# Split-weight slots of 4,128 bytes in place of 4,096 in a one-core encoder layer

## The chip, the core and the metric

The kernel runs on one core of a Trainium2 chip. The metric is the device time of one execution in microseconds, of which the median over several runs is given; lower is better. A matmul of this kernel is one TensorE (PE) instruction with a stationary operand of up to 128 x 128 elements, loaded ahead of it by an instruction that the profile keeps apart as PEld, and a moving operand of up to 512 columns.

## What is computed

One layer of an encoder over 256 tokens with 2,048 features, in float32:

```python
x = LN(ALPHA * x + 0.5 * swiglu(x, ffn1_w_gate, ffn1_w_up, ffn1_w_down))     # 2048 -> 5632 -> 2048
x = LN(ALPHA * x + (sigmoid(x @ w_gate[0] + b_gate[0]) * (diff_attention(x) @ w_branch_a)
                    + sigmoid(x @ w_gate[1] + b_gate[1]) * (dsa_attention(x) @ w_branch_b)) @ w_mix_out)
x = LN(ALPHA * x + memory_attention(x, mem))                                 # 4 heads over 256 memory tokens
x = LN(ALPHA * x + 0.5 * swiglu(x, ffn2_w_gate, ffn2_w_up, ffn2_w_down))
```

where `swiglu(x, g, u, d) = (silu(x @ g) * (x @ u)) @ d`. Nearly all of the work is products of 256 tokens with weight matrices that are read once from HBM.

## The kernel before, in words

Every product is made of float32r matmuls. To keep float32 accuracy each operand is split into a high part and a low part, and each product is the sum of three matmuls (`mm3`, lines 172 to 175): high times high (L173), high of the activations times low of the weights (L174), and low of the activations times high of the weights (L175). The activations, transposed (tile `xT`, or `hh` and `hl`, `ring`, `memT`, `mq`), are the stationary operand, 128 x 128. The weights (tiles `whi` and `wlo`) are the moving operand, 512 columns of them.

The weights come in units of 128 partitions x 1,024 float32, which is two k-tiles of 512 columns. SP loads a unit into one of four `raw` tiles (line 182), ACT copies it to `whi` with rounding to float32r (line 169), and DVE writes `wlo = raw - whi` (line 170). A split unit lies in a slot, a pair of `whi` and `wlo`, until both token tiles have used it: 2 token tiles x 2 k-tiles x 3 matmuls, 12 in all. There are six slots in the pool `wspl` throughout, four more in the pool `wx1` during the first feed-forward and two more in `wx2` during the second. `Feed` decides in program order which slot the next unit takes (the first pool with a free one) and how far ahead it is split. The order of all instructions is written out by the program (`manual_schedule`); nothing reorders them.

The tiles of a pool lie one behind the other in each partition of SBUF, and pools lie one behind the other too: `base` (with `xT`), `wraw` (`raw`), `wspl`, `stat`, and behind that the tiles of the current stage. So the length of a slot's tile sets the start address of every tile behind it. A slot's two tiles are 1,024 x 4 = 4,096 bytes each, a multiple of 256.

Of the kernel before, what the change touches and what calls it, by code (L numbers as in the profile page):

```python
# [16 lines left out]
P = 128  # L17
# [30 lines left out]
class Task:  # L48
    """Emission of a chain of dependent instructions in steps, between products."""

# [33 lines left out]
class Feed:  # L84
    """The weight units in the order of their use: loaded and split ahead of it."""

# [38 lines left out]
    def pump(self, count=99):  # L125
        """Splits ahead, while there is room."""
        while count and self.nsplit < len(self.plan):
            if self.plan[self.nsplit][3] is None and not any(self.slots.values()):
                return
            if self.nth[self.nsplit] > self.pulled + min(AHEAD, RAMP[0] + self.pulled // RAMP[1]):  # L130
                return
            self._split()
            count -= 1
# [16 lines left out]
def tile_encoder_layer(ctx, tc, a, out):  # L150
# [25 lines left out]

# [1 line left out]
    def load(src, width, cut):  # L178
# [8 lines left out]
    def split_unit(raw, width, into, cut, slot):  # L187
        if into is not None:
            hi, lo = into()
            raw = raw.rearrange("p (k t) -> p k t", t=T)  # L190
            w = 4 // cut
        else:
            hi = spl_pools[slot].tile([P, UNIT], F32R, name="whi")
            lo = spl_pools[slot].tile([P, UNIT], F32R, name="wlo")
            w = width // cut
        for i in range(cut):
            c = slice(i * w, (i + 1) * w)
            split(hi[:, c], lo[:, c], raw[:, c])
        return hi, lo
# [5 lines left out]
    @contextmanager  # L205
    def more_slots(name, bufs):
        """More room for split units, inside; its last ones are in use by then, and none is taken."""
        with tc.tile_pool(name=name, bufs=bufs) as pool:
            spl_pools[name] = pool
            feed.slots[name] = bufs  # L210
            yield
# [71 lines left out]
    def product(lhs, w, n, kts, lead=0, trail=0, after=None):  # L283
        """The two token tiles of lhs[K, tokens].T @ W[:, chunk n], over k-tiles kts of W: token tile 0
        ahead of tile 1 by `lead` units at the start and by `trail` at the end."""
        dst = [acc(), acc()]
        nu = len(kts) // KT
        held = {}

        def half(t, i):  # L290
            if i not in held:
                held[i] = feed.pull((w, n, kts[i * KT][1] // KT))
            unit_mm(lhs, dst, held[i], [kts[i * KT + j][0] for j in range(KT)], t, i == 0, i == nu - 1)
            if t == 1:
                feed.free(held.pop(i))
                if i < lead:
                    feed.pump(1)
                elif i - nu + trail == 1:
                    feed.pump(1)
            if i == nu - 1 and after is not None:  # L300
                after(t, dst[t])

        for t in range(2):
            for i in range(lead):
                half(t, i)
                tasks.tick()
        for i in range(lead, nu - trail):
            half(0, i)
            half(1, i)
            tasks.tick()  # L310
        for t in range(2):
            for i in range(nu - trail, nu):
                half(t, i)
                tasks.tick()
        return dst
# [8 lines left out]
    def rsqrt(dst, src, scale, eps):  # L324
        """dst = (src * scale + eps) ** -0.5"""
        w = src.shape[-1]
        v = stat.tile([P, 8], F32, name="rsq")
        nc.vector.tensor_scalar(v[:, :w], src, scale, eps, op0=ALU.mult, op1=ALU.add)
        nc.gpsimd.tensor_tensor(dst, v[:, :w], neg_half[:, :w], ALU.pow)  # L329

    def blocks_T(src, width=NCOL):
        """The transposes of src's 128-column blocks."""
        p = tp()
        for b in range(width // P):
            nc.tensor.transpose(p[:, b * P:(b + 1) * P], src[:, b * P:(b + 1) * P], ident)  # L335
        return p

    def transposed(src, hi, lo, width=NCOL):
        """hi + lo = the transposes of src's 128-column blocks."""
        p = blocks_T(src, width)[:, :width]  # L340
        split(hi, lo, p.rearrange("p (b t) -> p b t", t=P) if len(hi.shape) == 3 else p)
# [13 lines left out]

# [1 line left out]
    def ln_vectors(pool, i):  # L357
# [20 lines left out]
    def gain_bias_T(dst, p, i, n):  # L378
        """dst = p's blocks, a feature to a partition, times the gain, plus the bias of layer norm i."""
        for b in range(4):  # L380
            k = 2 * i * KD + 4 * n + b
            bs = slice(b * P, (b + 1) * P)
            nc.scalar.activation(dst[:, bs], p[:, bs], AF.Identity, scale=lnT[:, k:k + 1],
                                 bias=lnT[:, k + KD:k + KD + 1])

    def ln_task(y, t, sts, i, xT, gb, scratch, keep, kinds, pause, stride):
        """y's tile t <- its layer norm i; xT <- the norm, transposed and split. A chunk gets its gain
        and bias before the transposes (A) or, a feature to a partition, behind them (B)."""
        mv, rstd = ln_moments(sts)
# [55 lines left out]
    def store_task(y, t, sts, i, gb, scratch):  # L445
        """The last layer norm of y's tile t, stored: three chunks on DVE, one on ACT and TensorE."""
        mv, rstd = ln_moments(sts)
# [32 lines left out]

# [1 line left out]
    def ffn(pre, pool, y, xT, sts, lead, end):  # L482
        """y <- ALPHA * y + 0.5 * SwiGLU(x); end(t) follows the last product of token tile t."""
        for gi, (c0, c1) in enumerate(FFN_GROUPS):
# [39 lines left out]

# [1 line left out]
    x1_dram = dram.tile([P, 2, D], F32, name="x1_dram")  # L526
# [39 lines left out]

# [1 line left out]
    with tc.tile_pool(name="att", bufs=1) as att:  # L568
# [6 lines left out]
        def cols_T(p, scale, wait=0):  # L575
            """A product's token tiles, transposed: [feature, block, token]."""
            r = ring()
# [13 lines left out]
        def rows(p):  # L591
            """A product's token tiles as they are: [token, tile, column]."""
            r = ring().rearrange("p s b t -> p s (b t)")
            for t in range(2):
                s = slice(t * NCOL, (t + 1) * NCOL)
                split(r[:, 0, s], r[:, 1, s], p[t])
            return r
# [38 lines left out]
        def softmax_exp(dist, slope, p):  # L636
            """exp(logits - their maximum) and the sums, for both token tiles."""
            e = att.tile([P, 384], F32, name="e", bufs=4)
# [9 lines left out]
        def probs_T(e):  # L648
            """[key, (keys 0-127: 256 tokens | keys 128-255: tokens 128-255)]"""
            pT = att.tile([P, 2, 384], F32R, name="pT", bufs=2)  # L650
            transposed(e, pT[:, 0, :], pT[:, 1, :], 384)
            return pT

# [1 line left out]
        def diff_head(q, k, v, b, g, r):  # L655
# [43 lines left out]
        def heads(head, args, count, period, after):  # L699
            """Starts a head every `period` steps, once the tasks `after` are through."""  # L700
            while not all(t.done for t in after):
# [25 lines left out]

# [1 line left out]
        iq0, _ = cols_T(w_in(9), 1.0)  # L729
# [61 lines left out]

# [1 line left out]
        cT = ring()  # L793
# [21 lines left out]
        def latents(g):  # L815
            """Keys [feature, head, token] and values [token, tile, (head, feature)] of heads 4g..4g+3."""
            k = ring()
# [17 lines left out]

# [1 line left out]
        def dsa_head(q, k, v, b, g, r):  # L837
# [25 lines left out]

# [1 line left out]
        def y_lhs(yT):  # L865
# [68 lines left out]
    with tc.tile_pool(name="mem", bufs=1) as pool:  # L934
# [20 lines left out]

# [1 line left out]
        def cols_T2(p, scale, name):  # L957
# [58 lines left out]

# [1 line left out]
    with more_slots("wx2", MORE[1]), tc.tile_pool(name="ffn2", bufs=1) as pool:  # L1018
# [51 lines left out]
def _units(w):  # L1070
    """[K, N] -> [N chunk, K group, partition, (k-tile, column)]"""
    k, n = w.shape
# [4 lines left out]
def _columns(x):  # L1077
    """[tokens, K] -> [partition, (k-tile, token)]"""
    t, k = x.shape
# [52 lines left out]
```

## Time and profile before

| what | value |
|---|---|
| median of three runs | 2293.91 us (2292.02 to 2294.64) |
| span of the profiled execution, first to last instruction | 2291.1 us |
| PE busy in the span | 2273.7 us, 99%, 10,408 matmuls |
| PEld busy | 1866.6 us, 81% |
| DVE busy | 1283.5 us, 56% |
| ACT busy | 1031.0 us, 45% |
| mean granted TensorE clock | 0.998 |
| HBM traffic | 431.29 MB read, 190 GB/s over the span |

The profiled execution has no time of its own beside its span. The span is 2.8 us under the median of the runs, which also hold the start and the end around it. Matmuls are pipelined: one lasts some 390 ns by its record, and the next starts long before it ends. So for PE the time from one start to the next counts, and not the duration.

### The profile page before, as it was taken

To read this page: it belongs to the slowest core of one execution; us is meant where nothing else is said; L and a number is where in the kernel's file an instruction comes from. 1 tells how busy PE (TensorE), PEld (TensorE's weight loads), DVE (VectorE), ACT (ScalarE), POOL (GpSimd) and SP (SyncE) were. 2 spreads that over 40 slices of the span, in tenths; PEclk is the share of its full clock that TensorE was granted. 3 is DMA by queue.
4 is the path that set the end of the run, shared out by engine and by line. 5 is a ranking of instruction groups with operands and counts; after the bars stand their busy time and mean duration, and the time that the engine had idled before them with its cause. 6 is when DMAs were issued, how large, how long until landed. Compare 5 with 4: busy or idle time off the path is not lost.

```text
span 2291.1 us, 27032 instructions
## 1 busy us (share of the span) xinstructions
PE 2273.7 (99%) x10408; PEld 1866.6 (81%) x10408; DVE 1283.5 (56%) x1458; ACT 1031.0 (45%) x1317; POOL 22.0 (1%) x36
## 2 busy tenths in 40 slices
PE   9999999999999999999999999999999999999998
PEld 7888888888888888888888888878888888888886
DVE  5544544554455766685655556786445445454554
ACT  5443344434443555655544444655443444434442
POOL 0000000000000100000000000000000000000000
PEclk9999999999999999999999999999999999999999
DMA  8866666666665655445566677547666666666662
GB/s 269 285 201 187 190 189 187 188 189 188 190 184 168 211 156 175 141 147 172 183 191 206 199 240 245 173 159 223 188 227 186 191 187 191 184 190 189 187 186 93
DMA packets 120592, 437.25 MB, mean 191 GB/s; under 512 B 13504, under 2 KB 13632, under 8 KB 119312
## 3 DMA queue, kind: packets, MB, share of 16 engines
q1 hardware_dynamic: 119520, 431.02, 60.9%
q0 software_dynamic: 944, 4.52, 0.6%
q8 instruction: 81, 1.33, 0.2%
q14 instruction: 47, 0.39, 0.1%
HBM read 431.29 MB, written 4.19 MB: 190 GB/s over the span
## 4 chain that ended last, share of the span: by engine, by line
PE 98%; issue 1%; DVE 1%; ACT 0%; DMA 0%; POOL 0%; SPq 0%; POOLq 0%; ACTq 0%
PE acc L173 31%; PE acc L175 31%; PE acc L174 31%; PE tp L335 2%; PE tp L173 1%; PE tp L174 1%; PE tp L175 0%; DMA raw<-in_ffn_w_gate 0%; ACT me L985 0%; DVE nm L981 0%; DVE wlo L170 0%; ACT whi L169 0%; POOL rstd L329 0%; DVE sts L479 0%; DVE y L477 0%
## 5 line engine op out<-in xcount | busy, mean ns | idle before, releaser
L170 DVE TENSOR_TENSOR wlo<-raw,whi 128x1024 fp32r<-128x1024 f32 (+1 forms) x787 | 959.1, 1222 | 861.8 <-ACT whi L169 856.6
L169 ACT CAST whi<-raw 128x1024 fp32r<-128x1024 f32 (+1 forms) x787 | 822.4, 1049 | 957.1 <-PE acc L175 910.4
L173 PE MATMUL acc<-whi,xT 128*128 128x512 f32 x2176 | 857.3, 394 | 2.0 <-ACT whi L169 2.0
L175 PE MATMUL acc<-whi,xT 128*128 128x512 f32 x2176 | 850.9, 391 | 0.0
L174 PE MATMUL acc<-wlo,xT 128*128 128x512 f32 x2176 | 850.4, 391 | 0.2 <-DVE wlo L170 0.2
L173 PEld LDWEIGHTS acc<-whi,xT 128*128 128x128 f32 x2176 | 409.0, 188 | 90.3 <-ACT whi L169 4.0
L175 PEld LDWEIGHTS acc<-whi,xT 128*128 128x128 f32 x2176 | 408.7, 188 | 88.4
L174 PEld LDWEIGHTS acc<-wlo,xT 128*128 128x128 f32 x2176 | 409.2, 188 | 87.0 <-DVE wlo L170 1.4
L173 PE MATMUL acc<-whi,hh 128*128 128x512 f32 x704 | 277.6, 394 | 0.0
L175 PE MATMUL acc<-whi,hl 128*128 128x512 f32 x704 | 276.9, 393 | 0.0
L174 PE MATMUL acc<-wlo,hh 128*128 128x512 f32 x704 | 276.7, 393 | 0.0
L175 PEld LDWEIGHTS acc<-whi,hl 128*128 128x128 f32 x704 | 132.2, 188 | 30.6
L174 PEld LDWEIGHTS acc<-wlo,hh 128*128 128x128 f32 x704 | 132.2, 188 | 30.3
L173 PEld LDWEIGHTS acc<-whi,hh 128*128 128x128 f32 x704 | 132.2, 188 | 30.1
L173 PE MATMUL acc<-whi,ring 128*128 128x512 f32 x144 | 57.4, 398 | 0.0
L174 PE MATMUL acc<-wlo,ring 128*128 128x512 f32 x144 | 56.8, 395 | 0.0
L175 PE MATMUL acc<-whi,ring 128*128 128x512 f32 x144 | 56.8, 395 | 0.0
L477 DVE SCALAR_TENSOR_TENSOR y<-y,acc 128x512 f32<-128x512 f32 x64 | 42.2, 680 | 18.4 <-PE acc L175 18.3
L170 DVE TENSOR_TENSOR hl<-tp,hh 128x512 fp32r<-128x512 f32 x44 | 28.4, 686 | 33.5 <-ACT hh L169 33.5
L169 ACT CAST hh<-tp 128x512 fp32r<-128x512 f32 x44 | 23.7, 590 | 49.0 <-PE tp L335 49.0
L644 ACT ACTIVATE e<-e,nm 128x128 f32<-128x128 f32 (+1 forms) x48 | 21.5, 448 | 45.6 <-DVE nm L643 44.6
L500 ACT ACTIVATE silu<-acc 128x512 f32<-128x512 f32 x44 | 26.2, 599 | 22.7 <-PE acc L175 22.6
(194 smaller groups left out, 1097.7 us busy)
## 6 DMA issues: line engine op xcount, KB each, us to landing
raw<-in_ffn_w_up SPq DMA_DIRECT2D x176, 512.0 KB, 4.2
raw<-in_ffn_w_down SPq DMA_DIRECT2D x176, 512.0 KB, 3.8
raw<-in_ffn_w_gate SPq DMA_DIRECT2D x175, 512.0 KB, 4.1
raw<-in_w_in SPq DMA_DIRECT2D x88, 512.0 KB, 3.6
raw<-in_w_gate SPq DMA_DIRECT2D x64, 512.0 KB, 4.2
raw<-in_w_mix_out SPq DMA_DIRECT2D x32, 512.0 KB, 4.2
raw<-in_w_branch_a SPq DMA_DIRECT2D x16, 512.0 KB, 4.1
raw<-in_w_branch_b SPq DMA_DIRECT2D x16, 512.0 KB, 4.2
```

The costliest lines, as they stand in the source:

```text
L169: nc.scalar.copy(hi, src)
L170: nc.vector.tensor_tensor(lo, src, hi.bitcast(F32), ALU.subtract)
L173: nc.tensor.matmul(dst, lh, rh, start=start, stop=False)
L174: nc.tensor.matmul(dst, lh, rl, start=False, stop=False)
L175: nc.tensor.matmul(dst, ll, rh, start=False, stop=stop)
L335: nc.tensor.transpose(p[:, b * P:(b + 1) * P], src[:, b * P:(b + 1) * P], ident)
L477: nc.vector.scalar_tensor_tensor(c, c, scale, d, op0=ALU.mult, op1=ALU.add)
L500: nc.scalar.activation(s[t], g[t], AF.Silu)
L644: nc.scalar.activation(e[:, s0:s1], e[:, s0:s1], AF.Exp, bias=nm[:, t:t + 1], accum_out=sm[:, t:t + 1])
```

## The change

The two tiles of a slot become eight float32 (32 bytes) longer per partition, and only the first 1,024 elements are used, as before:

```diff
-            hi = spl_pools[slot].tile([P, UNIT], F32R, name="whi")
-            lo = spl_pools[slot].tile([P, UNIT], F32R, name="wlo")
+            hi = spl_pools[slot].tile([P, UNIT + 8], F32R, name="whi")[:, :UNIT]
+            lo = spl_pools[slot].tile([P, UNIT + 8], F32R, name="wlo")[:, :UNIT]
```

The rest of the diff takes out docstrings and comments. On every engine the instructions, their order and their waits are the same in both programs; only start addresses differ. Below, the place of a tile is its start address within a partition modulo 256, as the two programs lay their tiles out:

| tile | place before | place after |
|---|---|---|
| `xT`, `raw` | 160 | 160 |
| `whi` in `wspl`, six slots | 160 each | 160, 192, 224, 0, 32, 64 |
| `wlo` in `wspl`, six slots | 160 each | 96, 128, 160, 192, 224, 0 |
| `whi` in `wx1`, four slots | 32 each | 160, 192, 224, 0 |
| `wlo` in `wx1`, four slots | 32 each | 32, 64, 96, 128 |
| `whi` / `wlo` in `wx2`, two slots | 32 each | 160, 192 / 224, 0 |
| `hh`, `hl` of the first feed-forward | 32 | 160 |
| `hh`, `hl` of the second | 32 | 160 or 32 |
| `ring`, `memT`, `mq` | 32 | 160 |
| `ident`, the moving operand of transposes | 128 | 128 |

The 128-column blocks of the stationary tiles and the 512-column halves of the slots start at multiples of 256 from the tile's start, so a place holds for all of them. The distance of a matmul is the place of its moving operand minus that of its stationary operand, modulo 256. Counted over the 9,360 matmuls whose moving operand is 512 columns of a split weight:

| distance | 0 | 32 | 64 | 96 | 128 | 160 | 192 | 224 |
|---|---|---|---|---|---|---|---|---|
| before | 6036 | 0 | 0 | 0 | 3324 | 0 | 0 | 0 |
| after | 1556 | 1556 | 1412 | 1444 | 1060 | 1060 | 628 | 644 |

## Rows read from the trace of the kernel before

**Rows 1.** The page, its first line, parts 1 and 4.
```profile
span 2291.1 us, 27032 instructions
PE 2273.7 (99%) x10408; PEld 1866.6 (81%) x10408; DVE 1283.5 (56%) x1458; ACT 1031.0 (45%) x1317; POOL 22.0 (1%) x36
PE 98%; issue 1%; DVE 1%; ACT 0%; DMA 0%; POOL 0%; SPq 0%; POOLq 0%; ACTq 0%
```

**Rows 2.** The page, part 5: three groups of matmuls, with the idle time before them.
```profile
L173 PE MATMUL acc<-whi,xT 128*128 128x512 f32 x2176 | 857.3, 394 | 2.0 <-ACT whi L169 2.0
L175 PE MATMUL acc<-whi,xT 128*128 128x512 f32 x2176 | 850.9, 391 | 0.0
L174 PE MATMUL acc<-wlo,xT 128*128 128x512 f32 x2176 | 850.4, 391 | 0.2 <-DVE wlo L170 0.2
```

**Rows 3.** Two stretches of the mixers; columns: start:end, length, busy time and instructions by engine, PEclk, DMA.
```profile
1230.05:1241.21 11.16, 11.16 (x50) 9.05 (x49) 6.12 (x7) 5.31 (x6) 0.00 (x0) 1.00 0.60 181
1241.21:1262.98 21.77, 21.77 (x98) 18.02 (x97) 12.28 (x13) 8.43 (x8) 0.00 (x0) 1.00 0.69 207
```

**Rows 4.** The same view, two stretches of each feed-forward.
```profile
325.10:369.22 44.12, 44.12 (x196) 36.07 (x194) 22.09 (x20) 18.72 (x20) 0.00 (x0) 1.00 0.63 190
459.91:545.85 85.94, 85.94 (x376) 69.91 (x374) 43.08 (x40) 33.31 (x33) 0.00 (x0) 1.00 0.64 189
1856.04:1899.99 43.95, 43.95 (x195) 36.08 (x194) 22.09 (x20) 18.74 (x20) 0.00 (x0) 1.00 0.64 191
1990.35:2076.61 86.26, 86.26 (x376) 69.95 (x375) 43.09 (x40) 33.31 (x33) 0.00 (x0) 1.00 0.63 189
```

**Rows 5.** The timeline of PE and PEld, a moment in the second stretch of rows 3.
```profile
1252.09 0.39 PE L173 MATMUL acc<-whi,xT 128*128 128x512 f32 x1
1252.09 0.19 PEld L174 LDWEIGHTS acc<-wlo,xT 128*128 128x128 f32 x1
1252.32 0.39 PE L174 MATMUL acc<-wlo,xT 128*128 128x512 f32 x1
1252.32 0.19 PEld L175 LDWEIGHTS acc<-whi,xT 128*128 128x128 f32 x1
1252.54 0.39 PE L175 MATMUL acc<-whi,xT 128*128 128x512 f32 x1
```

**Rows 6.** The timeline of PE, a moment in the first stretch of rows 3.
```profile
1235.63 0.39 PE L173 MATMUL acc<-whi,ring 128*128 128x512 f32 x1
1235.87 0.39 PE L174 MATMUL acc<-wlo,ring 128*128 128x512 f32 x1
1236.09 0.39 PE L175 MATMUL acc<-whi,ring 128*128 128x512 f32 x1
1236.32 0.40 PE L173 MATMUL acc<-whi,ring 128*128 128x512 f32 x1
```

**Rows 7.** Groups by line, DVE and ACT, 1175 to 1330 us (slots of `wspl` alone).
```profile
L170 DVE TENSOR_TENSOR wlo<-raw,whi 128x1024 fp32r<-128x1024 f32 x57 | 69.8, 1225 | 71.6 <-ACT whi L169 71.6
L169 ACT CAST whi<-raw 128x1024 fp32r<-128x1024 f32 x56 | 58.9, 1052 | 82.5 <-PE acc L175 80.7 <-ACT whi L169 1.8
```

**Rows 8.** The same view, 1857 to 1987 us (slots of `wspl` and `wx2`).
```profile
L170 DVE TENSOR_TENSOR wlo<-raw,whi 128x1024 fp32r<-128x1024 f32 x47 | 57.6, 1225 | 63.1 <-ACT whi L169 62.8
L169 ACT CAST whi<-raw 128x1024 fp32r<-128x1024 f32 x48 | 50.5, 1052 | 67.7 <-PE acc L175 67.7
```

## The prediction

> **What bounds the kernel now.** I read the page first. PE is busy 99% of the span of 2291.1 us, and the chain that ended last runs through PE for 98% of it [rows 1]. Then the groups by line: ahead of the three largest groups of matmuls PE stood idle 2.0, 0.0 and 0.2 us in all [rows 2], so the splits and the loads of the weights are ahead of their use. Nothing that ACT, DVE or SP do ends last. What sets the time is how often PE starts a matmul, and so the view that matters is the stretch with its count: length over number of starts is the step from one matmul to the next.
>
> Two neighbouring stretches of the mixers differ in nothing but the tile that the stationary operand comes from [rows 3]. In the second one, 96 matmuls (of the 98 two are still draining from before) take the gate's weights against `xT`, both at place 160, distance 0: 21.77 us / 96 = 226.8 ns a step. In the first, 48 matmuls (of 50) take the branch's weights against `ring`, place 32, distance 128: 11.16 / 48 = 232.5 ns. The granted clock is 1.00 in both, the upper level of 2.4 GHz, and no engine is near full beside PE. The step is thus 5.7 ns longer at distance 128. The timeline shows where the two operands can meet: the load of the next stationary operand starts within 0.01 us of the matmul before it and runs 0.19 of its 0.23 us beside it [rows 5]. And it shows that distance 0 is steady (0.23, 0.22 in hundredths), while at distance 128 single steps go from 0.24 to 0.22 and 0.23 [rows 6].
>
> A rule of the Trainium skill speaks against any effect, and is the first rival below. (SBUF — State Buffer, the section on who interferes with whom: PE has two read ports, one for the moving operand and one for the load of weights, independent of each other, and waits on nobody. By it both stretches should step alike; the trace has 226.8 and 232.5 ns and does not agree.)
>
> **The change part by part.** No instruction is added, removed or moved, and no wait; neither do the queues of SP and POOL change. Four things could cost or give something.
>
> *The moving operand's place.* This is the term that counts. The number of matmuls at each distance stands in the table of the change. Before, by the steps just read: 6036 x 226.8 = 1368.9 us and 3324 x 232.5 = 772.8 us, 2141.7 us. After, 1556 stay at distance 0 (352.9 us), 1060 are at 128 (246.5 us), and 6744 are at six distances that the trace of before does not hold for a 512-column matmul. Their step x is unknown. Its near bounds are the two means, 226.8 and 232.5 ns; its far bounds are the single steps at distance 128, 0.22 and 0.24 us [rows 6]. I take the middle of the near bounds, 229.6 ns, as nothing puts the six nearer to either: 6744 x 229.6 = 1548.4 us. Sum after: 2147.8 us, 6.1 us more than before. One could hope for more: distance 0 is the cheaper of two, and it loses 4,480 of its matmuls.
>
> *The mixing.* Where slots at different distances alternate, the step is longer than the shares say. In the feed-forwards the slots of `wspl` and of `wx1` or `wx2` lie 128 apart. Of 192 matmuls of the first stretch 72 are at distance 128, which gives 228.9 ns; measured are 44.12 / 192 = 229.8. Of 372 of the second 216: 230.1 expected, 231.0 measured. Of 192 of the third 48: 228.2 and 228.9. Of 372 of the fourth 276: 231.0 and 231.9 [rows 4]. So mixing costs 0.7 to 0.9 ns a matmul, say 0.9. Before, it is paid on the 6,336 matmuls of the two feed-forwards (each 2 x 11 x 96 + 4 x 264): 5.7 us. After, it is paid on all 9,360: 8.4 us. That is 2.7 us more. After, the distance also changes between the matmuls of one unit, since `whi` and `wlo` lie at different places; before it changed only from unit to unit. So the price may be double, 1.8 ns: then the change here is 16.8 - 5.7 = 11.1 us.
>
> *Splits.* ACT and DVE take 1052 and 1225 ns for a unit where all slots lie at the place of `raw` [rows 7], and the same 1052 and 1225 ns where some lie 128 away [rows 8]. They are also covered: DVE is idle 44%, ACT 55% of the span [rows 1]. I cost them at nothing. If the cover went, a unit's 12 matmuls of 229 ns (2.7 us) still leave 1.5 us beside the 1.2 us of DVE.
>
> *The other tiles that are shifted.* The 1,046 remaining matmuls (10,408 less 9,360 and the two of the start) are transposes and attention products. If each shifted by the 5.7 ns between the two known distances, that would be 6 us either way. The attention products of `ring` with `ring` keep their distance, as both move together; the transposes against `ident` do not. I take 0 and keep 3 us either way.
>
> The sum is 6.1 + 2.7 = 8.8 us over the profiled span, 2299.9 us, and over the median of 2293.91 us it gives **2303 us**. About 0.2% (4.6 us) is what a measurement of this kernel can tell from no change. Break-even lies at x = 228.3 ns; below 227.6 ns the change is faster by over 0.2%, above 229.0 slower.
>
> The ends: before, products and mixing are 2141.7 + 5.7 = 2147.4 us. With x = 226.8 and mixing at 0.9 they are 2137.3 after, 10 us less; without any mixing 2128.9, 18 us less. With x = 232.5 and mixing at 1.8 they are 2184.2, 37 us more.
>
> The Trainium skill has a price for a step without any of this (TensorE: Matmul & The Clock Gate, back-to-back matmuls of 512 columns at the upper level of the clock: 215.7 ns). With it for all 9,360 the sum would fall by some 128 us; no row here comes near it, and the shortest single step is 0.22 us.
>
> **The rivals.** *No change* (22%). The difference in rows 3 may belong to the tile and not to the distance, or the six distances may average within 0.7 ns of 228.3. For it: the known distances lie on both sides of 228.3, so an average over many lands near. Against the first half: stretches with `xT` alone become longer with the share at distance 128 [rows 3, 4]. Time: 2289 to 2298 us. By the skill's rule above the result would be this one.
>
> *Faster* (28%). The two known distances are both multiples of 128; the places between could keep the load of the next stationary operand and the moving operand out of each other's way better than either. Place: every matmul of the gates, `w_in`, `w_mix_out` and the feed-forwards. Price: with x = 226.8 it is 10 us less, 2284 us; with x = 224 ns, between that and the shortest single step, 6744 x 5.6 = 38 us under the forecast, 2265 us. It decides once x is under 227.6 ns. For it: single steps of 0.22 us exist. Against it: they stand beside longer ones.
>
> *Much slower* (5%). The steady step at distance 0 may be a lucky lock, and x nearer to the long single steps of 0.24 us: 6744 x (238 - 229.6) = 57 us over the forecast, 2360 us. For it: only distance 0 shows steady steps. Against it: no stretch of the trace averages above 232.5 ns by more than mixing.
>
> *The change does not do what it says.* The program's addresses exclude it: the slots take all eight places, though not equally often, and distances 192 and 224 get 628 and 644 matmuls against 1,556 at 32.
>
> **How the numbers follow.** The forecast, a step between the two known ones with mixing, has 45%, no change 22%, faster 28%, much slower 5%. Slower by over 0.2% is the forecast and the last, 50%. The range goes from x = 226.8 without mixing (-18 us) to x = 232.5 with double mixing (+37 us), with 3 us at each end for the shifted tiles: 2272 to 2334 us. It leaves out the much slower case and the better half of the faster one. The likeliest case alone spans 2299 to 2334 us.
>
> **What would show it right or wrong.** In the profile after, PE still has 99% and the groups of rows 2 no more idle time; the durations on DVE and ACT stay at 1225 and 1052 ns. The gate's stretch of 96 matmuls goes from 21.77 us to about 22.1 (230.5 ns a step), and the branch's 48 go from 11.16 down to about 11.06. The steps within one unit differ, as `whi` and `wlo` have their own distances. If the gate's stretch stays at 21.8 us or falls, the forecast is wrong in its middle distances; if it goes over 22.4, the known two were no bound. If waits of PE on ACT or DVE appear, the cover that I assumed was not there.

## The result, and the profile after

| | before | after |
|---|---|---|
| median | 2293.66 us (4 runs) | 2316.27 us (4 runs, 2315.62 to 2317.21) |
| span of the profiled execution | 2291.1 us | 2313.7 us |

The changed kernel is slower: the ratio is 1.0102, with a 95% interval of 1.0087 to 1.0116. The direction is the one forecast, and 2316 us lies inside the range of 2272 to 2334; but the loss is 22.6 us, two and a half times the 8.8 us that were worked out.

The page of the changed kernel has the same picture of engines as [rows 1]: its first line, the engines' busy time, the chain by engine, and the three groups of [rows 2].

```profile
span 2313.7 us, 27032 instructions
PE 2296.3 (99%) x10408; PEld 1867.2 (81%) x10408; DVE 1283.4 (55%) x1458; ACT 1029.7 (45%) x1317; POOL 22.0 (1%) x36
PE 98%; DVE 1%; issue 1%; ACT 0%; DMA 0%; POOL 0%; POOLq 0%; SPq 0%; ACTq 0%
L173 PE MATMUL acc<-whi,xT 128*128 128x512 f32 x2176 | 864.0, 397 | 2.2 <-ACT whi L169 2.2
L174 PE MATMUL acc<-wlo,xT 128*128 128x512 f32 x2176 | 858.3, 394 | 0.2 <-DVE wlo L170 0.2
L175 PE MATMUL acc<-whi,xT 128*128 128x512 f32 x2176 | 857.5, 394 | 0.0
```

The whole difference of 22.6 us in the span is on PE's busy time (2296.3 less 2273.7). DVE's busy time moved by 0.1 us and ACT's by 1.3, downwards, and PE waits no longer than before: 2.2, 0.2 and 0.0 us ahead of the three groups. So PE does not wait for anything that the profile shows as a wait; its steps are longer.

The stretches after that answer to [rows 3], then to [rows 4], in the same view (start:end, length, busy time and instructions by engine, PEclk, DMA):

```profile
1242.05:1253.16 11.11, 11.11 (x49) 9.02 (x48) 6.04 (x7) 5.32 (x6) 0.00 (x0) 1.00 0.63 184
1253.16:1275.43 22.27, 22.27 (x97) 18.03 (x96) 12.34 (x13) 8.39 (x8) 0.00 (x0) 1.00 0.68 204
328.23:372.84 44.61, 44.61 (x196) 36.10 (x195) 22.09 (x20) 18.68 (x20) 0.00 (x0) 1.00 0.61 188
464.36:550.69 86.33, 86.33 (x376) 69.95 (x375) 43.15 (x40) 33.33 (x33) 0.00 (x0) 1.00 0.63 188
1874.61:1919.21 44.60, 44.60 (x195) 36.09 (x194) 22.09 (x20) 18.68 (x20) 0.00 (x0) 1.00 0.63 188
2010.77:2096.99 86.22, 86.22 (x375) 69.95 (x374) 43.17 (x40) 33.34 (x33) 0.00 (x0) 1.00 0.63 189
```

The same 96 matmuls of a gate take 22.27 us where they took 21.77: 232.0 ns a step for 226.8. The 48 of a branch go the other way, 11.16 to 11.11 us, 231.5 ns for 232.5. In the feed-forwards the stretches against `xT` grow from 44.12 and 43.95 to 44.61 and 44.60 us (232.3 ns), while those against `hh` and `hl` move less: 85.94 to 86.33 (231.0 to 232.1 ns, over 372 matmuls), and 86.26 to 86.22 (231.9 to 231.8). So every stretch now has a step of 231.5 to 232.3 ns, whatever its stationary tile, and the loss is where distance 0 was common. The granted clock is 1.00 in all of them, the level of 2.4 GHz as before.

### The profile page after: what moved, and what is told of

Read it like the earlier page. It is cut to its first block, busy times and chain, and to the rows that moved or that the text cites. A ratio compares the mean times of both kernels' runs of the same rounds, so it can differ in the third digit from the quotient of the medians.

```text
span 2313.7 us, 27032 instructions
## 1 busy us (share of the span) xinstructions
PE 2296.3 (99%) x10408; PEld 1867.2 (81%) x10408; DVE 1283.4 (55%) x1458; ACT 1029.7 (45%) x1317; POOL 22.0 (1%) x36
## 4 chain that ended last, share of the span: by engine, by line
PE 98%; DVE 1%; issue 1%; ACT 0%; DMA 0%; POOL 0%; POOLq 0%; SPq 0%; ACTq 0%
PE acc L173 31%; PE acc L174 31%; PE acc L175 31%; PE tp L335 2%; PE tp L173 1%; PE tp L174 1%; PE tp L175 1%; DMA raw<-in_ffn_w_gate 0%; DVE wlo L170 0%; ACT whi L169 0%; ACT me L985 0%; DVE nm L981 0%; POOL rstd L329 0%; DVE sts L479 0%; DVE y L477 0%
## 5 line engine op out<-in xcount | busy, mean ns | idle before, releaser
L173 PE MATMUL acc<-whi,xT 128*128 128x512 f32 x2176 | 864.0, 397 | 2.2 <-ACT whi L169 2.2
L174 PE MATMUL acc<-wlo,xT 128*128 128x512 f32 x2176 | 858.3, 394 | 0.2 <-DVE wlo L170 0.2
L175 PE MATMUL acc<-whi,xT 128*128 128x512 f32 x2176 | 857.5, 394 | 0.0
L173 PEld LDWEIGHTS acc<-whi,xT 128*128 128x128 f32 x2176 | 409.3, 188 | 97.3 <-ACT whi L169 3.9
L175 PEld LDWEIGHTS acc<-whi,xT 128*128 128x128 f32 x2176 | 409.2, 188 | 95.8
L174 PEld LDWEIGHTS acc<-wlo,xT 128*128 128x128 f32 x2176 | 409.1, 188 | 93.5 <-DVE wlo L170 1.4
L173 PE MATMUL acc<-whi,hh 128*128 128x512 f32 x704 | 277.8, 395 | 0.0
L174 PE MATMUL acc<-wlo,hh 128*128 128x512 f32 x704 | 277.2, 394 | 0.0
L175 PE MATMUL acc<-whi,hl 128*128 128x512 f32 x704 | 277.0, 393 | 0.0
L175 PEld LDWEIGHTS acc<-whi,hl 128*128 128x128 f32 x704 | 132.2, 188 | 30.8
L173 PEld LDWEIGHTS acc<-whi,hh 128*128 128x128 f32 x704 | 132.3, 188 | 30.4
L174 PEld LDWEIGHTS acc<-wlo,hh 128*128 128x128 f32 x704 | 132.2, 188 | 30.5
L173 PE MATMUL acc<-whi,ring 128*128 128x512 f32 x144 | 57.3, 398 | 0.0
L174 PE MATMUL acc<-wlo,ring 128*128 128x512 f32 x144 | 56.9, 395 | 0.0
L175 PE MATMUL acc<-whi,ring 128*128 128x512 f32 x144 | 56.6, 393 | 0.0
```

Source lines behind the costliest of these rows:

```text
L173: nc.tensor.matmul(dst, lh, rh, start=start, stop=False)
L174: nc.tensor.matmul(dst, lh, rl, start=False, stop=False)
L175: nc.tensor.matmul(dst, ll, rh, start=False, stop=stop)
```

## The experiments

All of them keep the slots' length of before but one (`len256`), keep all instructions in order, and only move start addresses. Unless said otherwise a kernel was timed once beside a run of the kernel before, which took 2292.9 to 2295.3 us.

### All 9,360 matmuls at distance 0, 128 and 64

One parameter `DIST` and unused tiles of some bytes (`pad`) ahead of the slots, behind `stat`, and around the pools of the stages put every slot at place 160 + `DIST` and every stationary tile at 160:

```diff
+    pad(ctx, DIST)
     wspl = ctx.enter_context(tc.tile_pool(name="wspl", bufs=SPL))
...
+    pad(ctx, 128)
...
-    with more_slots("wx1", MORE[0]), tc.tile_pool(name="ffn1", bufs=1) as pool:
+    with more_slots("wx1", MORE[0]), padded((256 - DIST) % 256), tc.tile_pool(name="ffn1", bufs=1) as pool:
...
-    with tc.tile_pool(name="att", bufs=1) as att:
+    with padded((256 - DIST) % 256), tc.tile_pool(name="att", bufs=1) as att:
...
+    pad(ctx, (256 - DIST) % 256)
     res = ctx.enter_context(tc.tile_pool(name="res", bufs=1))
...
-    with more_slots("wx2", MORE[1]), tc.tile_pool(name="ffn2", bufs=1) as pool:
+    with padded(DIST), more_slots("wx2", MORE[1]), padded((256 - DIST) % 256), tc.tile_pool(name="ffn2", bufs=1) as pool:
```

`DIST = 0`, the median of four runs:

> The slots keep their length of before; pads move the other tiles so that all 9,360 matmuls of split weights are at distance 0. Distance theory (the step depends on the distance and is steady where it stays the same): every step 226.8 ns as in the gate stretch of before, no mixing; the branch stretch of 48 matmuls falls from 11.16 to 10.9 us, and the whole from 2294 to about 2294 - 3324 x 5.7 ns - 5.7 us = 2269 us. Tile theory (the step belongs to the stage's stationary tile, not to its place): nothing moves, 2294 us.

Measured: 2272.69 us, a ratio of 0.9907 to the kernel before (0.9890 to 0.9923). This is the distance theory's 2269 us within 4 us; the tile theory's 2294 us falls. The branch and the gate of this kernel, and the first feed-forward's two stretches, in the same view:

```profile
1285.25:1296.13 10.88, 10.88 (x50) 9.01 (x48) 6.06 (x7) 5.34 (x6) 0.00 (x0) 1.00 0.59 186
1296.13:1317.89 21.76, 21.76 (x98) 18.02 (x96) 12.33 (x13) 8.44 (x8) 0.00 (x0) 1.00 0.65 206
321.89:365.53 43.64, 43.64 (x196) 36.09 (x194) 22.09 (x20) 18.77 (x20) 0.00 (x0) 1.00 0.62 192
455.16:539.58 84.42, 84.42 (x376) 69.93 (x375) 43.06 (x40) 33.52 (x33) 0.00 (x0) 1.00 0.64 192
```

The branch, which had 232.5 ns against `ring`, now has 10.88 / 48 = 226.7 ns against the same tile at another place. The feed-forward's stretches fall to 43.64 / 192 = 227.3 ns and 84.42 / 372 = 226.9 ns. So the first of them keeps half a nanosecond over the 226.8 that was expected, though no distance alternates any more.

`DIST = 128`:

> As before in slots' length, with pads so that all 9,360 matmuls are at distance 128. Distance theory: every step 232.5 ns, the gate stretch of 96 becomes 22.3 us, the whole 2147.4 -> 2176 us in these matmuls, about 2323 us. Tile theory: 2294 us, gate stretch 21.77 us.

Measured: 2321.36 us, within 2 us of the distance theory's 2323. The step in the gate is 22.30 / 96 = 232.3 ns (its row stands with those of the other distances). The first feed-forward's two stretches:

```profile
328.05:372.93 44.88, 44.88 (x196) 36.08 (x195) 22.07 (x20) 18.67 (x20) 0.00 (x0) 1.00 0.60 187
464.70:551.23 86.53, 86.53 (x376) 70.18 (x374) 43.14 (x40) 33.32 (x33) 0.00 (x0) 1.00 0.62 188
```

They step 44.88 / 192 = 233.8 ns and 86.53 / 372 = 232.6 ns, again with one distance throughout.

`DIST = 64`:

> As before in slots' length, with pads so that all 9,360 matmuls are at distance 64. If a distance has its own price whatever lies around it, the step is the 231 ns that the changed kernel shows on average at distance 64, and the whole about 2310 us. If what costs is that the distance changes from matmul to matmul, a steady 64 is as good as a steady 0: 227 ns, about 2269 us.

Measured: 2290.56 us, between the two, and the gate's step is 21.97 / 96 = 228.9 ns. Neither reading held as written: a steady 64 is not as good as a steady 0, nor does it cost the 231 ns that it has on average among other distances.

### Longer slots that keep their places

```diff
-            hi = spl_pools[slot].tile([P, UNIT], F32R, name="whi")
+            more = 64 if slot == "wspl" else 0
+            hi = spl_pools[slot].tile([P, UNIT + more], F32R, name="whi")[:, :UNIT]
```

> The whi tiles of the six wspl slots are 256 bytes longer, so every address behind them moves and every place stays. Distance theory: no change, within 0.2% of 2294 us. If the length of the slot or the address itself mattered, slower, towards the 2316 us of the change.

Measured: 2294.63 us beside 2294.47 us for the kernel before. Tiles that are longer by 256 bytes, and addresses that move by multiples of 256, do nothing here; what the other runs changed is the place modulo 256.

### The other distances, steady

> All 9,360 matmuls at a steady distance of 32. Own-price theory (each distance has a step of its own, and the change pays their average): the six distances that before lacked average about 231.5 ns, and 32 is one of the dear ones by its average of 232.4 ns in the changed kernel: about 2272.7 + 9360 x 5.4 ns = 2323 us. Mixing theory (a steady distance is cheaper than the same one among others): under 230 ns, at most 2300 us.

> All at a steady 96. Own-price theory: 234.0 ns as in the changed kernel, the dearest, about 2337 us. Mixing theory: under 230 ns, at most 2300 us.

> All at a steady 160. Own-price theory: 232.3 ns as in the changed kernel, about 2322 us. Mixing theory: under 230 ns, at most 2300 us.

> All at a steady 192. Own-price theory: 230.9 ns as in the changed kernel, about 2309 us. Mixing theory: near 229 ns like 64, whose steady step was 229.1 ns against 231.1 in the changed kernel, about 2291 us.

> All 9,360 at a steady 224, the last distance of the eight. Own-price theory: near 233 ns, as 232.9 was the average at 224 in the changed kernel and 32, 96 and 192 had 233.3: gate stretch of 96 at 22.4 us, the whole about 2329 us. Mixing theory: under 230 ns, at most 2300 us.

Measured: 2329.46, 2331.99, 2337.38, 2329.66 and 2329.71 us. The mixing theory falls at each of them, and these five are the dear ones. The own-price theory's numbers came from averages over the changed kernel's trace (weighted by the table of the change they give 232.4 ns for the six distances, not the 231.5 of the expectation for 32). They were met at 224, too low at 32 (2323), 160 (2322) and 192 (2309), and a little high at 96 (2337): a distance that stays is not its own average among others, but none of these five came near 2300. The stretch of the gate (96 matmuls) in each kernel, `DIST` = 32, 64, 96, 128, 160, 192 and 224, in this order:

```profile
1327.29:1349.69 22.40, 22.40 (x98) 18.00 (x96) 12.34 (x13) 8.39 (x8) 0.00 (x0) 1.00 0.66 202
```
```profile
1305.51:1327.48 21.97, 21.97 (x97) 18.03 (x96) 12.33 (x13) 8.38 (x8) 0.00 (x0) 1.00 0.67 207
```
```profile
1329.63:1352.03 22.40, 22.40 (x97) 18.02 (x96) 12.35 (x13) 8.39 (x8) 0.00 (x0) 1.00 0.66 204
```
```profile
1322.60:1344.90 22.30, 22.30 (x97) 18.08 (x96) 12.32 (x13) 8.39 (x8) 0.00 (x0) 1.00 0.67 204
```
```profile
1332.02:1354.51 22.49, 22.49 (x97) 18.08 (x96) 12.33 (x13) 8.40 (x8) 0.00 (x0) 1.00 0.64 203
```
```profile
1327.37:1349.77 22.40, 22.40 (x97) 18.05 (x96) 12.34 (x13) 8.39 (x8) 0.00 (x0) 1.00 0.67 202
```
```profile
1327.64:1350.04 22.40, 22.40 (x97) 18.03 (x96) 12.34 (x13) 8.40 (x8) 0.00 (x0) 1.00 0.68 205
```

DVE's and ACT's work in these stretches is the same to some hundredths of a microsecond, and so is the clock. Length over 96 gives the price of each steady distance in the gate:

| distance | 0 | 32 | 64 | 96 | 128 | 160 | 192 | 224 |
|---|---|---|---|---|---|---|---|---|
| step, ns | 226.7 | 233.3 | 228.9 | 233.3 | 232.3 | 234.3 | 233.3 | 233.3 |
| whole kernel, us | 2272.7 | 2329.5 | 2290.6 | 2332.0 | 2321.4 | 2337.4 | 2329.7 | 2329.7 |

Distance 0 is the cheapest of the eight and 64 the only other one that is not dear. The moving operand's place alone does not decide: at place 160 it has 226.8 ns against `xT` and 232.5 against `ring` [rows 3]. In all these kernels the stationary tiles start at place 160. Whether the distance alone counts or the pair of places was thus compared only at 128, where 160 against 32 (`ring` before) has 232.5 ns and 32 against 160 (`DIST` = 128) has 232.3; at the other distances it is not shown.

### Half a place

`xT` 16 bytes lower modulo 256, by a longer tile of which the first 60 elements are left free (`Halves` returns the two halves of `xT` as views at given offsets):

```diff
-        return base.tile([P, 2, KD, T], F32R, name="xT")
+        return Halves(base.tile([P, 2 * KD * T + 60 + 4], F32R, name="xT"), 60, 0)
```

> As d0, but xT starts 16 bytes lower modulo 256, so that its 6,528 products have distance 16. If the price goes by whole places of 32 bytes, the step stays 226.7 ns and the whole 2273 us. If it goes by the exact start, something between 226.7 and the 233.3 ns of distance 32: in the middle 230 ns, about 2294 us.

Measured: 2276.96 us, 4 us over distance 0. The gate's stretch is the same 21.76 us, but the product with `w_mix_out` (360 matmuls) takes 82.29 us where distance 0 has 81.70. Its rows here, and below it the one of distance 0:

```profile
1298.13:1319.89 21.76, 21.76 (x97) 18.02 (x96) 12.34 (x13) 8.42 (x8) 0.00 (x0) 1.00 0.69 207
1339.72:1422.01 82.29, 82.29 (x364) 67.63 (x362) 50.27 (x49) 36.38 (x36) 0.58 (x1) 1.00 0.80 272
```
```profile
1337.73:1419.43 81.70, 81.70 (x364) 67.68 (x362) 50.21 (x49) 36.56 (x36) 0.58 (x1) 1.00 0.79 273
```

226.7 ns in one stage and 228.6 in another, at one distance, where distance 0 has 226.7 and 226.9. So 16 bytes are nearly free over the whole kernel, but the step is not a function of the distance alone. What sets the one or the other was not tried.

### One half of the stationary tile moved

The low half of `xT` alone, and then the high half alone, at distance 32, the rest at 0 (`pad(ctx, 32)` ahead of the slots goes with the first). The first added line is the low half's kernel, the second the high half's:

```diff
-        return base.tile([P, 2, KD, T], F32R, name="xT")
+        return Halves(base.tile([P, 2 * KD * T + 0 + 56], F32R, name="xT"), 0, 56)
+        return Halves(base.tile([P, 2 * KD * T + 56 + 8], F32R, name="xT"), 56, 8)
```

> As d0, but the low half of the tile xT is moved so that the products of the low half of the activations (L175) have distance 32, and the 4,352 others of xT keep 0. If the price hangs on the moving operand and the load of the next stationary operand beside it, the step after L174 becomes long, since the low half is loaded during it, and the one after L175 stays short. If it hangs on a matmul's own two operands, the step after L175 becomes long. Either way about 2176 x 6.6 ns = 14 us over d0, 2287 us. If place of neither matters while the slots are steady: 2273 us.

> The mirror of lo32: the high half of xT is at distance 32 (L173 and L174, 4,352 products), the low half at 0 (L175, 2,176). In the mixers, if the load beside a matmul decides, the steps after L173 and L175 are the long ones (a high half is loaded beside them) and L174 the shortest; if a matmul's own pair decides, L173 and L174 are long and L175 the shortest. By the prices of steady distances the whole is 2272.7 + 4352 x 6.6 ns = 2301 us; if one distance among others disturbs its neighbours as in lo32 (14 ns for each one moved), up to 2330 us.

Measured: 2303.82 us with the low half moved, 31 us over distance 0, twice what was expected; 2312.05 us with the high half moved, 39 us over it, in the expected span. The gate's stretches are these, the low half's kernel first:

```profile
1314.12:1336.31 22.19, 22.19 (x97) 18.02 (x96) 12.40 (x13) 8.39 (x8) 0.00 (x0) 1.00 0.66 206
```
```profile
1317.93:1340.33 22.40, 22.40 (x97) 18.02 (x96) 12.42 (x13) 8.41 (x8) 0.00 (x0) 1.00 0.66 205
```

Mean step from a matmul's start to the next, over the 191 or 192 of each line against `xT` between 1140 and 1340 us, worked out from the starts in the trace (in each cell, the distances of the matmul's own pair and of the load beside it follow the mean in ns):

| own pair, load beside it | after L173 | after L174 | after L175 |
|---|---|---|---|
| low half at 32 | 228.4 (0, 0) | 234.3 (0, 32) | 232.2 (32, 0) |
| high half at 32 | 237.0 (32, 32) | 233.2 (32, 0) | 231.2 (0, 32) |

In the first kernel the load beside the matmul looks like the cause, in the second the matmul's own pair: the shortest step with one of them at 32 is L175's, where the load theory wanted L174's. Either one of the two lengthens the step, and both together lengthen it most. Which of them acts, or whether one long step shifts the next, stays open: the same (0, 32) has 234.3 ns in one kernel and 231.2 in the other.

## Why the prediction was right or wrong

**What bounds the kernel** held: PE is at 99%, and no wait took the place of anything. **Splits** held: in the same view as [rows 7], the changed kernel has 1225 and 1048 ns.

```profile
L170 DVE TENSOR_TENSOR wlo<-raw,whi 128x1024 fp32r<-128x1024 f32 x57 | 69.8, 1225 | 73.8 <-ACT whi L169 73.8
L169 ACT CAST whi<-raw 128x1024 fp32r<-128x1024 f32 x56 | 58.7, 1048 | 85.0 <-PE acc L175 83.0 <-ACT whi L169 2.0
```

**The mechanism**, a price on the moving operand's distance, was right in the main, and is shown by the kernels at distance 0 and 128 and the one with longer slots: the same tiles and instructions go from 2272.7 to 2321.4 us by places alone, and a longer slot at its old place does nothing. What makes a step longer at one distance than at another is not shown. The rule of the Trainium skill that was weighed against it (SBUF — State Buffer, the section on who interferes with whom: PE's two read ports are independent and PE waits on nobody) does not describe these steps: they run from 226.7 to 234.3 ns with the distance.

**The step that failed** is the size of x, the mean step of the six unknown distances, put at 229.6 ns, "as nothing puts the six nearer to either" bound. The steady kernels give 233.3 (32), 228.9 (64), 233.3 (96), 234.3 (160), 233.3 (192) and 233.3 ns (224). Weighted by the 6,744 matmuls of the change that is 232.5 ns: the upper of the two near bounds, and five of the eight distances lie above 233 ns. The term is thus 6744 x 232.5 = 1568 us in place of 1548.4, some 20 us more. With it and the prediction's other prices the products alone would rise by 25.9 us. The two distances of before were no sample from the middle: distance 0, which carried most of the matmuls, is the cheapest of the eight, and what left it paid more.

**That each distance keeps its price among others** was a second error, and the total does not show it. If each matmul in the changed kernel's trace is given the distance that it has when the program takes its slots in turn, the step after one at distance 0 averages 232.3 ns over all stages; the kernel with distance 0 throughout averages 227.9 (steps over 330 ns left out in both). So the 1,556 matmuls that the prediction left at 226.8 ns became some 4 ns dearer, about 7 us in all. By the same reading the six other distances average 232.5 ns in the changed kernel and 233.5 in their steady kernels, some 6 us less, and the two nearly cancel.

**The mixing** was misread in part. The prediction took the excess of the feed-forwards' stretches over their shares, 0.7 to 0.9 ns, for a cost of alternating distances. But the kernels with one distance throughout have an excess in these stretches too. Their own steps, 227.3 at distance 0 and 233.8 at 128 in the first stretch, give 229.7 ns for its 120 and 72 matmuls, and the kernel before has 229.8: nothing is left for mixing. In the second, 226.9 and 232.6 give 230.2 ns for 156 and 216, and 231.0 were measured: 0.8 is left. In the changed kernel, by the steady prices and its own distances, the gate would step 231.7 ns and steps 232.0; the branch 231.1 and 231.5. That is 0.3 to 0.4 ns, not 0.9, although the distance now changes within a unit.

The whole kernels say the same. The eight times of the table of steady distances, weighted by the counts in the table of the change, give 2290.0 us for the kernel before and 2314.6 for the changed one, 24.6 us apart; measured are 2293.7 and 2316.3. What the mixture adds to the steady prices is thus an estimated 3.7 us before and 1.7 after: 2 us less, where the prediction had 2.7 us more. Single runs of the kernel before differ by up to 3.3 us (2292.02 to 2295.3), so this 2 us is a sign and no more.

The direction was in part luck: the midpoint of 229.6 ns lay only 1.3 ns above break-even, and the prediction itself gave slower no more than 50%.

**The signs named in advance**: the gate's stretch went to 22.27 us where 22.1 was forecast and 22.4 was the limit; the branch fell to 11.11 (forecast 11.06); the single steps in the gate, all 226 to 233 ns before, run from 226 to 237. **The rivals**: *faster* falls, as none of the six new distances is under 228.3 ns. *Much slower* needed a mean near 238 ns and did not come; its reason, that the steady step at 0 is a special one, fits the 232.3 ns that distance 0 has among others, but x came nowhere near 238. *No change* falls with x at 232.5, and its first half, that the difference belongs to the tile, with the branch at distance 0: the same `ring` steps 226.7 ns there.

## What to carry to other kernels

Where a kernel is held by back-to-back matmuls, compare the step of stretches that differ only in a tile, by length over count: here waits, clock and busy shares showed nothing, and the step showed 2.5%. Then look at where the tiles start. Putting all moving and stationary operands at one place modulo 256 by a single unused tile of 128 bytes made this kernel 0.93% faster than before (2272.69 us), where spreading the slots over all places made it 1.0% slower. When only two of eight values of a price are known, the middle of the two is no estimate of the others: try one uniform value per run, since a change that mixes eight at once shows only their mean.

## What the runs showed of the hardware that was not expected

- The step of a 512-column float32r matmul against a 128 x 128 stationary operand depends on the start addresses modulo 256: in the gate, 226.7 ns at distance 0, 228.9 at 64, 232.3 to 234.3 at the six others, all at a granted clock of 1.00.
- A steady distance does not cost the same in every stage: 128 has 232.3 ns in the gate and 233.8 in the first feed-forward's stretch against `xT`; 0 has 226.7 and 227.3. Why is not shown.
- The price does not add up by shares: 2,176 of the 9,360 matmuls at distance 32 cost 31 us (14 ns each), all 9,360 at 32 cost 57 us (6 ns each).
- ACT's and DVE's work over the same tiles hardly depended on the places: in the gate's stretch 8.38 to 8.44 us and 12.32 to 12.35 us at all eight distances.
